# Three tiles of their own for two of a pair's seven split operands, and the last row tile's sums put ahead of the early products

## The chip, the cores and the metric

The kernel runs on one core of one Trainium2 chip. The metric is the device time of one launch in microseconds (us). A core has a matrix engine, TensorE (PE; its weight loads are listed apart as PEld), VectorE (DVE), ScalarE (ACT), GpSimd (POOL), a sync engine (SP) that issues transfers, and DMA engines. Each takes its instructions in the order in which they were put into its queue, and waits by semaphores for what the others do. Tiles lie in on-chip memory (SBUF); PE writes into banks of PSUM, which DVE and ACT read.

## What is computed

One layer of an encoder for a sequence of 1024 rows of width 1024 in float32: a norm, an input projection, an S5 scan beside a Fourier mixer, an output projection, and then the part that the change touches, a gated feed-forward network with a convolution of width 3 along the sequence:

```
h = h + concat([y_ssm, y_fft]) @ w_out
up = rmsnorm(h, g_ffn) @ w_up                      # 1024 x 1024  @  1024 x 5632
conv = conv_b + sum_k conv_w[k] * shifted(up, k)   # k = 0, 1, 2
gate, val = split(conv, 2)
h = h + (gelu(gate) * val) @ w_down                # 1024 x 2816  @  2816 x 1024
out = rmsnorm(h, g_final)
```

## The kernel before

**Precision.** A float32 product is made of three matmuls on float32r operands: each operand is split into a high part (a copy on ACT, L151) and a low part (a subtraction, on DVE, L152, or on POOL where the code says so), and high x high, high x low and low x high are summed (`mm`, L130).

**The stage of the output projection (`rows`, R0 to R7).** Row tile s, 128 rows, is multiplied by `w_out`, added to h, and its sum of squares is taken. **The norm and its transpose (`columns`, C0 to C7)** scale row tile s, transpose it on PE (L1033, tiles `n2_s_pt`), and put it, split, into the operands of the up-projection: row tiles 0 to 3 into `B11` and `B21` (tile `xa`); row tiles 4 to 7 into sums with the row tile four places ahead of them (L1049 to L1053) and from there into `T1` (tile `t1o`), `T2` (`t2o`), `T3` and `B22` (`xb`) and `T4` (`t4o`). The split into T4 is on POOL, that into T1 too, except for the last row tile.

**The up-projection (`up_pair`, 22 pairs j).** Pair j is 128 columns of the gate and the 128 of the value, with 1024 rows. Its four blocks are worked out with seven products in place of eight, after Strassen and Winograd: `weights(j)` loads four blocks `wu` of `w_up`, makes from them three sums `ws` on DVE (L1083, L1084, L1086; a fourth, L1085, goes into a `wu` tile), and splits the seven operands 0 to 6 (A11, S2, A12, A21, S1, A22, S4) into tiles `wo{j}_0` to `wo{j}_6`. Each product is 12 matmuls of 128x512, so a pair has 84. Products 0 and 2 go into bank `u1`, 1 into `u2`, 3 and 5 into `u3`, 4 and 6 into `u4`. DVE and ACT add the banks up (L1116, L1119, L1137 to L1147), convolve (L1099, L1102), apply gelu (L1150) and multiply (L1151), and SP writes the result to memory as `adr{j}`.

**Early products (`early_pair`, E0 to E4).** For pairs 0 to 4, products 0 and 2 need `xa` alone, that is row tiles 0 to 3. They are made ahead, from operands `we{j}_0` and `we{j}_1`, while the last row tiles are still normed; these pairs then have 60 matmuls left. Results are kept in `ug{j}`; those of pairs 2 to 4 lie in the ring of `wd_tile`.

**Buffers.** A ring is a set of buffers that tiles of one tag take in turn; who wants one waits until the readers of its old tile are done. All split operands of `w_up` (tag `wp`) share a ring of five (`NWP`), the blocks as loaded (tag `st`) one of five, and the sums `ws` one of three. `wd_tile` is a ring of three tiles of the size of a split operand. Blocks of `w_out` lie in it, then `ug2` to `ug4`; after pair 4 it is idle until `load_first`, which is called ahead of pair 21 and loads and splits six blocks for the down projection (`first0` to `first5`), the last two into this ring.

**Order.** `SEQ2` says in which order R, C and E are written. The order of each engine's queue is then made by a scheduler that plans with a timeline of its own: a changed line can move instructions at other places too, and pairs interleave (products 2, 5 and 6 of pair j are run by PE inside pair j + 1).

After the 22 pairs the down projection runs (banks `pd`), two halves of four row tiles.

Of the kernel before, what the change touches and what calls it, by code (L numbers as in the profile page):

```python
# [12 lines left out]
F32R = mybir.dt.float32r  # L13
# [7 lines left out]
P = 128  # L21
# [12 lines left out]
NWP = 5  # L34
# [1 line left out]
NTAB = 1026  # L36
NT4 = 9
MODE = "x"
SEQ2 = "R0 R1 C0 R2 C1 R3 C2 R4 C3 R5 C4 R6 R7 E0 C5 E1 C6 E2 E3 E4 C7"


ON = {
# [47 lines left out]
def encoder_block(  # L90
# [8 lines left out]
    V, A, PE, GP = nc.vector, nc.scalar, nc.tensor, nc.gpsimd  # L99
# [5 lines left out]
    outer = ctx.enter_context(tc.tile_pool(name="outer", bufs=1))  # L105
# [44 lines left out]
    def split(dst_hi, dst_lo, src, eng=V):  # L150
        A.activation(dst_hi, src, AF.Copy)  # L151
        return eng.tensor_sub(dst_lo, src, dst_hi.bitcast(F32))  # L152
# [759 lines left out]
    def w_out_block(part, n, k, dst=None):  # L912
        r0 = part * 512 + k * P
        return load_split(w_out[0][r0:r0 + P, n * 512:(n + 1) * 512], 1, f"wo{part}_{n}_{k}", dst,
                          opt(f"wo{part}{n}{k}", V))
# [44 lines left out]
    def raw(name):  # L960
        return x16.tile([P, 512], F32, name=name, tag="ra", bufs=3)

    def wd_tile(name):
        return fp.tile([P, 2, 512], F32R, name=name, tag="wd", bufs=3)
# [32 lines left out]
    wo = [[w_out_block(0, n, k, wd_tile(f"wot{n}_{k}") if n and k else None) for k in range(4)] for n in range(2)]  # L997
# [69 lines left out]
    def weight_block(j, i, kh, name):  # L1067
        c0 = i * D_FF + j * P
        t = outer.tile([P, 512], F32, name=name, tag="st", bufs=5)
        st_load(nc.sync.dma_start(t.rearrange("p (k c) -> p k c", k=4),  # L1070
                                  w_up[0][:, c0:c0 + P].rearrange("(k p) c -> p k c", p=P)[:, 4 * kh:4 * kh + 4]))
        return t

    def operand(t, name, e=V):
        w = outer.tile([P, 2, 512], F32R, name=name, tag="wp", bufs=NWP)
        split(w[:, 0], w[:, 1], t, e)
        return w.rearrange("p t (k c) -> p t k c", k=4)

    def weights(j, early):

        A11, A12, A21, A22 = (weight_block(j, i, kh, f"wu{j}_{i}{kh}") for i in range(2) for kh in range(2))
        S1, S2, S4 = (raw(f"ws{j}_{i}") for i in (1, 2, 4))
        V.tensor_add(S1, A21, A22)  # L1083
        V.tensor_sub(S2, S1, A11)  # L1084
        V.tensor_sub(A21, A11, A21)  # L1085
        V.tensor_sub(S4, A12, S2)  # L1086
        return [None if early and i in (0, 2) else operand(t, f"wo{j}_{i}")
                for i, t in enumerate((A11, S2, A12, A21, S1, A22, S4))]

    def product(dst, w, xx, fresh, more=False):  # L1090
# [30 lines left out]
    def early_pair(j):  # L1121
        w11, w12 = (operand(weight_block(j, 0, kh, f"we{j}_{kh}"), f"we{j}_{kh}_o") for kh in range(2))
        done[j] = t4(f"ug{j}") if j < 2 else wd_tile(f"ug{j}").rearrange("p i c -> p (i c)").bitcast(F32)
        for _ in first_half(j, done[j], w11, w12):
            pass

    def up_pair(j):
        w11, w2, w12, w3, w1, w22, w4 = weights(j, j in done)
        b2, b3, b4 = bank(f"u2_{j}"), bank2(f"u3_{j}"), bank2(f"u4_{j}")
        cv = t4(f"uv{j}")  # L1130
        u2, p7 = halves(f"up_{j}")
        cg = done[j] if j in done else t4(f"ug{j}")
        if j not in done:
            fh = first_half(j, cg, w11, w12)
            next(fh)
        product(b2, w2, T2, True)
        V.tensor_add(u2, cg[:, 512:1024], b2)  # L1137
        if j not in done:
            next(fh, None)
        product(b3, w3, T3, True, True)  # L1140
        V.tensor_add(p7, u2, b3)
        product(b4, w1, T1, True, True)
        V.tensor_add(cv[:, 512:1024], p7, b4)
        product(b3, w22, T4, False, True)
        V.tensor_add(cv[:, 0:512], u2, b3)
        product(b4, w4, B22, False, True)
        V.tensor_add(cg[:, 512:1024], u2, b4)  # L1147
        g = conv(cg, j, f"cg{j}")
        v = conv(cv, NFF + j, f"cv{j}")
        A.activation(g, g, AF.Gelu_apprx_tanh)  # L1150
        V.tensor_mul(g, g, v)  # L1151
        nc.sync.dma_start(adr[j], g)

    steps = {"R": rows, "C": columns, "E": early_pair}
    for tok in SEQ2.split():
        n2_end = steps[tok[0]](int(tok[1:]))
# [146 lines left out]
```

## Time and profile before

| | |
|---|---|
| time, median of 3 runs | 1111.56 us (1110.78 to 1112.57) |
| the profiled execution | 1111.17 us, its span 1109.4 us |
| mean clock granted to PE | 0.971 of full speed |
| early products and last row tiles | up to about 452 us |
| pairs 0 to 21 | about 447 to 867 us |
| down projection | about 867 us to the end |

A timeline row has the start in us, the duration in us, the engine, the line, the operation, the tiles as output<-inputs (buffer numbers left out, so `wo10_0` is `wo`), the shape and how many instructions the row joins; in brackets how long the engine was idle before it, and who released it.

The rows of the queues that are shown with the change have no times; where they carry names in full, `wo10_0_5475` is operand 0 of pair 10 (the last number is a mere count).

### The profile page before, as it was taken

Reading aid. Unit: us, or ns where it says so; the run is one execution under the profiler, and the core shown is the slowest. Engines: PE = TensorE matmul, PEld = TensorE weight load, DVE = VectorE, ACT = ScalarE, POOL = GpSimd, SP = SyncE. Lnnn points to the kernel's source line nnn. Section 1 sums busy time; section 2 is a strip of 40 time slices with the busy share of each in tenths; the row PEclk is TensorE's granted clock in tenths of the full one; section 3 lists DMA queues with packets and bytes.
Section 4 is the critical chain, followed back from the end, with each engine's and each line's share of the span. In section 5 each row is a group of like instructions: output and inputs, shape, how many; then the busy total and the mean of one; then the engine's idle time right before and its main releaser. Section 6 shows DMA issues by size and latency. Waiting matters only on the chain.

```text
span 1109.4 us, 13600 instructions
## 1 busy us (share of the span) xinstructions
PE 1005.3 (91%) x4636; PEld 820.9 (74%) x4636; DVE 869.2 (78%) x1599; ACT 449.4 (41%) x819; POOL 232.2 (21%) x245
## 2 busy tenths in 40 slices
PE   2799887788799997899999999999989999999997
PEld 1677765666678886688777777777768788888885
DVE  6998989999897898699887887878887733483335
ACT  5443232532126464344443434435344433353333
POOL 6257565775650022000000000000000000010002
PEclk9999888887999999899999999999999999999999
DMA  7251002431012332223222232222330774366521
GB/s 232 39 162 51 22 22 85 145 118 57 25 39 92 108 124 76 66 86 104 87 87 76 67 105 67 80 82 66 100 109 19 245 272 146 116 225 221 162 95 76
DMA packets 115259, 115.25 MB, mean 104 GB/s; under 512 B 17217, under 2 KB 85878, under 8 KB 115190
## 3 DMA queue, kind: packets, MB, share of 16 engines
q1 hardware_dynamic: 115046, 114.06, 32.4%
q8 instruction: 36, 0.59, 0.2%
q14 instruction: 33, 0.27, 0.1%
q10 hardware_dynamic: 144, 0.33, 0.1%
HBM read 91.82 MB, written 22.51 MB: 103 GB/s over the span
## 4 chain that ended last, share of the span: by engine, by line
PE 53%; DVE 4%; DMA 2%; ACT 1%; issue 1%; POOL 0%; POOLq 0%; DVEq 0%; ACTq 0%
PE u L130 31%; PE pd L130 21%; DMA wu<-in_w_up_dram 1%; DVE cg L1102 1%; DVE wo L152 1%; ACT wo L151 1%; DVE cv L1102 1%; ACT cg L1099 0%; DVE first L152 0%; DMA first_st<-adr 0%; DMA first_st<-in_w_down_dram 0%; DVE ws L1086 0%; DVE ug L1147 0%; DVE up L1137 0%; DVE ws L1084 0%
## 5 line engine op out<-in xcount | busy, mean ns | idle before, releaser
L130 PE MATMUL pd<-wd,at 128*128 128x512 f32 x1008 | 229.1, 389 | 2.6 <-ACT wd L151 1.6
L130 PEld LDWEIGHTS pd<-wd,at 128*128 128x128 f32 x1008 | 189.0, 188 | 42.6 <-ACT wd L151 2.0
L1201 POOL TENSOR_TENSOR o<-hb,gl 128x512 f32<-128x512 f32 (+1 forms) x10 | 13.4, 1343 | 640.6 <-DVE hb L1197 635.4
L130 PE MATMUL u<-xb,wo 128*128 128x512 f32 x528 | 130.2, 392 | 0.0
L130 PEld LDWEIGHTS u<-xb,wo 128*128 128x128 f32 x528 | 98.2, 188 | 24.0 <-DVE wo L152 4.0
L130 PE MATMUL u<-xa,wo 128*128 128x512 f32 x408 | 102.6, 394 | 6.7 <-ACT wo L151 5.6
L152 DVE TENSOR_TENSOR at<-at_st,at 128x512 fp32r<-128x512 f32 x42 | 29.0, 691 | 100.5 <-ACT at L151 100.4
L151 ACT ACTIVATE wo<-wu 128x512 fp32r<-128x512 f32 x78 | 49.3, 632 | 130.4 <-PE u L130 125.1
L130 PEld LDWEIGHTS u<-xa,wo 128*128 128x128 f32 x408 | 75.4, 188 | 28.1 <-ACT wo L151 11.1
L130 PE MATMUL pin<-xh,win 128*128 128x512 f32 x256 | 78.2, 406 | 1.1 <-ACT xh L224 1.1
L130 PE MATMUL u<-t2o,wo 128*128 128x512 f32 x264 | 69.3, 400 | 9.2 <-ACT t2o L151 8.3
L151 ACT ACTIVATE wo<-ws 128x512 fp32r<-128x512 f32 x66 | 41.3, 625 | 74.7 <-PE u L130 67.2
L130 PE MATMUL u<-t1o,wo 128*128 128x512 f32 x264 | 69.1, 391 | 1.8 <-ACT wo L151 1.8
L151 ACT ACTIVATE at<-at_st 128x512 fp32r<-128x512 f32 x42 | 26.4, 629 | 106.3 <-PE pd L130 97.7
L1102 DVE SCALAR_TENSOR_TENSOR cg<-ug,cw,cg 128x896 f32<-128x896 f32 (+1 forms) x88 | 62.0, 746 | 8.7 <-ACT cg L1099 8.7
L130 PEld LDWEIGHTS u<-t2o,wo 128*128 128x128 f32 x264 | 49.6, 192 | 22.6 <-ACT t2o L151 8.7
L130 PE MATMUL u<-t4o,wo 128*128 128x512 f32 x264 | 63.5, 389 | 0.0
L1102 DVE SCALAR_TENSOR_TENSOR cv<-uv,cw,cv 128x896 f32<-128x896 f32 (+1 forms) x88 | 62.0, 744 | 0.0
L130 PEld LDWEIGHTS u<-t1o,wo 128*128 128x128 f32 x264 | 49.2, 188 | 13.4 <-ACT wo L151 3.4
L130 PE MATMUL pwo<-wo,yf 128*128 128x512 f32 x192 | 52.0, 420 | 7.6 <-DVE h L928 4.3
L152 DVE TENSOR_TENSOR wo<-wu,wo 128x512 fp32r<-128x512 f32 x78 | 53.5, 685 | 5.9 <-ACT wo L151 5.8
L152 DVE TENSOR_TENSOR wd<-wd_st,wd 128x512 fp32r<-128x512 f32 x84 | 55.8, 698 | 2.4 <-ACT wd L151 2.3
(357 smaller groups left out, 1964.8 us busy)
## 6 DMA issues: line engine op xcount, KB each, us to landing
wu<-in_w_up_dram SPq DMA_DIRECT2D x88, 256.0 KB, 2.9
wd_st<-in_w_down_dram SPq DMA_DIRECT2D x84, 256.0 KB, 3.7
adr<-cg SPq DMA_DIRECT2D x22, 512.0 KB, 2.6
at_st<-adr SPq DMA_DIRECT2D x42, 256.0 KB, 3.9
xr<-in_x_dram SPq DMA_DIRECT2D x8, 512.0 KB, 8.1
win_st<-in_w_in_dram SPq DMA_DIRECT2D x16, 256.0 KB, 3.0
wo_st<-in_w_out_dram SPq DMA_DIRECT2D x16, 256.0 KB, 2.9
h<-in_x_dram SPq DMA_DIRECT2D x8, 512.0 KB, 4.6
```

Source lines behind the costliest of these rows:

```text
L130: i = PE.matmul(o, lhsT, rhs, start=start, stop=stop, skip_group_check=skip)
L151: A.activation(dst_hi, src, AF.Copy)
L152: return eng.tensor_sub(dst_lo, src, dst_hi.bitcast(F32))
L1102: V.scalar_tensor_tensor(cv[:, lo:hi], src[:, at:at + hi - lo], w, cv[:, lo:hi], ALU.mult, ALU.add)
L1201: GP.tensor_mul(o[:, sl], hv[:, sl], gl[:, sl])
```

## The change

Two edits:

```
-SEQ2 = "R0 R1 C0 R2 C1 R3 C2 R4 C3 R5 C4 R6 R7 E0 C5 E1 C6 E2 E3 E4 C7"
+SEQ2 = "R0 R1 C0 R2 C1 R3 C2 R4 C3 R5 C4 R6 R7 E0 C5 C6 C7 E1 E2 E3 E4"
```

```
-    def operand(t, name, e=V):
-        w = outer.tile([P, 2, 512], F32R, name=name, tag="wp", bufs=NWP)
+    def operand(t, name, w=None, e=V):
+        if w is None:
+            w = outer.tile([P, 2, 512], F32R, name=name, tag="wp", bufs=NWP)
         split(w[:, 0], w[:, 1], t, e)
         return w.rearrange("p t (k c) -> p t k c", k=4)
...
-        return [None if early and i in (0, 2) else operand(t, f"wo{j}_{i}")
+        return [None if early and i in (0, 2) else operand(t, f"wo{j}_{i}", wd_tile(f"wx{j}_{i}") if j > 4 and i in (1, 4) else None)
                 for i, t in enumerate((A11, S2, A12, A21, S1, A22, S4))]
```

The first writes the norm, transposes, sums and splits of row tiles 6 and 7 ahead of the early products of pairs 1 to 4. The second takes operands 1 and 4 (S2 and S1) of pairs 5 to 21 out of the ring of five and puts them, as `wx{j}_1` and `wx{j}_4`, into the ring of `wd_tile`. No operation is added or removed. Lines behind the edit have a number one higher after it. SP issues the same transfers; only `adr0` and two blocks of pair 21 change places with a neighbour, and POOL's queue has the same order.

**Where the queues differ: the last row tile.** On DVE, before, from the first sum of pair 1's weights (`ws_1_4263`) on; `n_7_pt` are row tile 7's transposes, `h_2712` and `h_2310` its sums:

```order
L1083 TENSOR_TENSOR ws_1_4263<-wu_10_4259,wu_11_4261 128x512
L152 TENSOR_TENSOR wo_4_4161<-ws_1_4148,wo_4_4161 128x512
L1085 TENSOR_TENSOR wu_10_4259<-wu_00_4255,wu_10_4259 128x512
L1084 TENSOR_TENSOR ws_2_4264<-ws_1_4263,wu_00_4255 128x512
L152 TENSOR_TENSOR wo_5_4164<-wu_11_4146,wo_5_4164 128x512
L1050 TENSOR_TENSOR h_2712<-n_7_pt_4114,h_2712 128x512
L1051 TENSOR_TENSOR h_2310<-n_7_pt_4120,h_2712 128x512
L1052 TENSOR_TENSOR h_2310<-n_7_pt_4120,h_2310 128x512
L152 TENSOR_TENSOR t1o<-h_2712,t1o 128x4x128
L152 TENSOR_TENSOR wo_6_4167<-ws_4_4150,wo_6_4167 128x512
L152 TENSOR_TENSOR t2o<-h_2310,t2o 128x4x128
```

The same place of DVE after the change, from the first sum of pair 0's weights (`ws_1_4148`) to the first of pair 1's, with rows of pair 0 left out between:

```order
L1084 TENSOR_TENSOR ws_1_4148<-wu_10_4144,wu_11_4146 128x512
L1050 TENSOR_TENSOR h_2712<-n_7_pt_3962,h_2712 128x512
L152 TENSOR_TENSOR t2o<-h_2465,t2o 128x4x128
...
L1051 TENSOR_TENSOR h_2310<-n_7_pt_3968,h_2712 128x512
L1052 TENSOR_TENSOR h_2310<-n_7_pt_3968,h_2310 128x512
...
L152 TENSOR_TENSOR t1o<-h_2712,t1o 128x4x128
...
L152 TENSOR_TENSOR t2o<-h_2310,t2o 128x4x128
...
L1084 TENSOR_TENSOR ws_1_4263<-wu_10_4259,wu_11_4261 128x512
```

Row tile 7's sums and its splits now stand ahead of pair 1's `ws`, mixed with row tile 6's. On PE the same place before, from the last products of the early pairs on:

```order
L130 MATMUL u1_3_4047<-xa_3367,we3_1_o_4043 128x512 x12
L130 MATMUL u1_4_4085<-xa_3367,we4_0_o_4076 128x512 x2
L1033 MATMUL n2_7_pt0_4114<-ident_70,n2_7_xs_4112 128x128
L1033 MATMUL n2_7_pt1_4120<-ident_70,n2_7_xs_4112 128x128 x4
L130 MATMUL u1_4_4085<-xa_3367,we4_1_o_4081 128x512 x12
L130 MATMUL u2_0_4170<-t2o_3172,wo0_1_4155 128x512 x12
L130 MATMUL u3_0_4171<-xb_3368,wo0_3_4158 128x512
L130 MATMUL u4_0_4172<-t1o_3370,wo0_4_4161 128x512 x12
L130 MATMUL u3_0_4171<-xb_3368,wo0_3_4158 128x512 x11
```

And after:

```order
L1033 MATMUL n2_7_pt0_3962<-ident_70,n2_7_xs_3960 128x128 x4
L1033 MATMUL n2_7_pt1_3968<-ident_70,n2_7_xs_3960 128x128 x4
L130 MATMUL u1_2_4037<-xa_3367,we2_1_o_4033 128x512 x12
L130 MATMUL u1_3_4075<-xa_3367,we3_0_o_4066 128x512
L130 MATMUL u1_4_4113<-xa_3367,we4_0_o_4104 128x512 x12
L130 MATMUL u1_3_4075<-xa_3367,we3_1_o_4071 128x512 x12
L130 MATMUL u2_0_4170<-t2o_3172,wo0_1_4155 128x512
L130 MATMUL u3_0_4171<-xb_3368,wo0_3_4158 128x512
L130 MATMUL u1_4_4113<-xa_3367,we4_1_o_4109 128x512 x12
L130 MATMUL u4_0_4172<-t1o_3370,wo0_4_4161 128x512 x2
L130 MATMUL u2_0_4170<-t2o_3172,wo0_1_4155 128x512 x11
```

The transposes have moved ahead of four early groups, and single matmuls of pair 0 (`u2_0`, `u3_0`) stand ahead of the last early product.

**A steady pair.** PE before, from the fifth product of pair 10 to the first of pair 11:

```order
L130 MATMUL u3_9_5348<-t4o_3369,wo9_5_5341 128x512 x12
L130 MATMUL u4_10_5498<-t1o_3370,wo10_4_5487 128x512 x8
L130 MATMUL u4_9_5349<-xb_3368,wo9_6_5344 128x512 x12
L130 MATMUL u4_10_5498<-t1o_3370,wo10_4_5487 128x512 x2
L130 MATMUL u1_11_5651<-xa_3367,wo11_0_5624 128x512 x2
L130 MATMUL u2_11_5645<-t2o_3172,wo11_1_5627 128x512 x2
```

And after:

```order
L130 MATMUL u3_10_5497<-xb_3368,wo10_3_5484 128x512 x10
L130 MATMUL u3_9_5348<-t4o_3369,wo9_5_5341 128x512 x12
L130 MATMUL u4_9_5349<-xb_3368,wo9_6_5344 128x512 x12
L130 MATMUL u1_11_5651<-xa_3367,wo11_0_5624 128x512 x2
L130 MATMUL u2_11_5645<-t2o_3172,wx11_1_5627 128x512 x12
```

The copy into `wo11_0` waits, before, for the product of `wo9_6`, whose buffer it takes, and PE has two matmuls of `u4_10` between that product and `u1_11`. After, it takes the buffer of `wo9_5`, and the twelve matmuls of `wo9_6` lie between. The copies of ACT for pair 12 before:

```order
L151 ACTIVATE wo11_6_5642<-ws11_4_5619 128x512
L151 ACTIVATE wo12_0_5773<-wu12_00_5758 128x512
L151 ACTIVATE wo12_1_5776<-ws12_2_5767 128x512
L1099 ACTIVATE cg10_5594<-ug10_5501,cw_107 128x1024
L1099 ACTIVATE cv10_5600<-uv10_5499,cw_107 128x1024
L1116 ACTIVATE ug11_5650<-u1_11_5651 128x512
L151 ACTIVATE wo12_2_5779<-wu12_01_5760 128x512
```

And after:

```order
L151 ACTIVATE wo11_6_5642<-ws11_4_5619 128x512
L151 ACTIVATE wx12_1_5776<-ws12_2_5767 128x512
L151 ACTIVATE wx12_4_5785<-ws12_1_5766 128x512
L151 ACTIVATE wo12_0_5773<-wu12_00_5758 128x512
L151 ACTIVATE wo12_2_5779<-wu12_01_5760 128x512
L1100 ACTIVATE cg10_5594<-ug10_5501,cw_107 128x1024
```

The copies of the sums, `wx12_1` and `wx12_4`, now stand ahead of `wo12_0`.

**Pair 20 and the first blocks of the down projection.** ACT before; `first` is the tile of blocks 0 to 3:

```order
L151 ACTIVATE first_7099<-first0_st_7102 128x512
L151 ACTIVATE first_7099<-first1_st_7106 128x512
L151 ACTIVATE wo20_0_6965<-wu20_00_6950 128x512
L151 ACTIVATE wo20_1_6968<-ws20_2_6959 128x512
L1099 ACTIVATE cg18_6786<-ug18_6693,cw_107 128x1024
```

And after:

```order
L151 ACTIVATE first_7099<-first0_st_7102 128x512
L151 ACTIVATE wo20_0_6965<-wu20_00_6950 128x512
L151 ACTIVATE wo20_2_6971<-wu20_01_6952 128x512
L151 ACTIVATE first_7099<-first1_st_7106 128x512
L1100 ACTIVATE cg18_6786<-ug18_6693,cw_107 128x1024
...
L151 ACTIVATE first_7099<-first2_st_7110 128x512
L151 ACTIVATE first_7099<-first3_st_7114 128x512
L151 ACTIVATE first0_7100<-first4_st_7118 128x512
L151 ACTIVATE wo20_3_6974<-wu20_10_6954 128x512
```

Pair 20's `wo20_0` has moved ahead of `first1`, and `wo20_3` now stands behind `first1` to `first4`.

## Prediction

> **What bounds the kernel now.** I read the busy shares first, then TensorE's (PE's) timeline around its idle times, then the engines that it waits for there.
>
> ```profile
> PE 1005.3 (91%) x4636; PEld 820.9 (74%) x4636; DVE 869.2 (78%) x1599; ACT 449.4 (41%) x819; POOL 232.2 (21%) x245
> ```
>
> PE is the bound: no other engine comes near its 91%. The change removes no matmul, so it can only win where PE waits. In the stretch that the change touches first, PE's timeline and its windows (columns: stretch, length, busy time of PE, weight loads, VectorE (DVE), ScalarE (ACT) and GpSimd (POOL), then the granted clock, the DMA share and GB/s) read:
>
> ```profile
> 433.12 0.71 PE L1033 MATMUL n_pt<-ident,n_xs 128*128 128x128 f32 x5
> 435.42 3.02 PE L130 MATMUL u<-xa,we_o 128*128 128x512 f32 x12 [1.60 <-ACT ug L1116]
> 446.69 0.79 PE L130 MATMUL u<-t2o,wo 128*128 128x512 f32 x1 [8.26 <-ACT t2o L151]
> 448.41 4.17 PE L130 MATMUL u<-t2o,wo 128*128 128x512 f32 x11 [0.92 <-DVE t2o L152]
> 452.41 0.39 PE L130 MATMUL u<-xb,wo 128*128 128x512 f32 x1
> ```
>
> ```profile
> 434.00:438.00 4.00, 2.58 (x11) 2.17 (x12) 2.31 (x3) 2.37 (x5) 0.56 (x1) 1.00 0.39 115
> 438.00:442.00 4.00, 0.43 (x2) 0.01 (x1) 1.24 (x3) 0.00 (x0) 0.00 (x0) 0.89 0.21 59
> 442.00:446.00 4.00, 0.00 (x0) 0.00 (x0) 3.90 (x8) 1.51 (x3) 0.67 (x1) 0.50 0.34 101
> 446.00:450.00 4.00, 2.39 (x5) 1.59 (x6) 4.00 (x5) 2.16 (x5) 1.87 (x2) 0.50 0.11 32
> ```
>
> PE finishes the last early product at 438.4 and idles 8.26 us for `t2o` of row tile 7, then 0.92 us for its low half, and the clock that follows the hole is 0.50. I call this the **transition**. VectorE's and GpSimd's timelines tell why:
>
> ```profile
> 429.25 1.78 DVE L152 TENSOR_TENSOR t2o<-h,t2o 128x512 fp32r<-128x512 f32 x1
> 430.94 0.68 DVE L1084 TENSOR_TENSOR ws<-ws,wu 128x512 f32<-128x512 f32 x1
> 431.55 0.68 DVE L1085 TENSOR_TENSOR wu<-wu,wu 128x512 f32<-128x512 f32 x1
> ...
> 440.76 0.69 DVE L1083 TENSOR_TENSOR ws<-wu,wu 128x512 f32<-128x512 f32 x1 [4.45 <-DMA wu<-in_w_up_dram]
> ...
> 443.77 0.68 DVE L1050 TENSOR_TENSOR h<-n_pt,h 128x512 f32<-128x512 f32 x1
> ...
> 447.67 0.68 DVE L152 TENSOR_TENSOR t2o<-h,t2o 128x512 fp32r<-128x512 f32 x1
> ```
>
> ```profile
> 428.74 1.73 POOL L1053 TENSOR_TENSOR h<-h,h 128x512 f32<-128x512 f32 x1
> ```
>
> Pair 1's `ws` waits 4.45 us for its weight DMA, in order, ahead of row tile 7's sums (L1050 at 443.77), whose inputs the PE had transposed by 433.83 (433.12 + 0.71).
>
> The second loss returns with **every pair** of the up-projection. A steady piece of PE's timeline, the copy of ScalarE that ends its wait, and the waits from 560 to 780:
>
> ```profile
> 649.81 0.74 PE L130 MATMUL u<-xa,wo 128*128 128x512 f32 x2 [0.27 <-ACT wo L151]
> ...
> 655.46 2.88 PE L130 MATMUL u<-xa,wo 128*128 128x512 f32 x12
> 658.18 3.08 PE L130 MATMUL u<-xb,wo 128*128 128x512 f32 x12
> ...
> 669.69 0.73 PE L130 MATMUL u<-xa,wo 128*128 128x512 f32 x2 [0.27 <-ACT wo L151]
> ```
>
> ```profile
> 669.00 0.63 ACT L151 ACTIVATE wo<-wu 128x512 fp32r<-128x512 f32 x1 [3.90 <-PE u L130]
> ```
>
> ```profile
> ACT wo L151 <- PE u L130: 113.7, 55, 4.1
> ```
>
> A period is 669.69 - 649.81 = 19.88 us. A product without a stall takes 658.18 - 655.46 = 2.72 us, 0.2267 us a matmul, so 84 matmuls could take 19.04: about 0.83 us is lost. The loss begins where PE needs `wo_0` of the next pair, whose copy ACT starts only at 669.00, since PE has just freed its slot. The four stretches after the transition, in windows:
>
> ```profile
> 468.70:540.60 71.90, 70.78 (x310) 57.72 (x309) 71.81 (x111) 35.19 (x45) 0.00 (x0) 1.00 0.30 95
> 452.41:570.25 117.84, 115.52 (x505) 94.12 (x503) 103.28 (x158) 48.97 (x66) 0.00 (x0) 1.00 0.27 85
> 570.25:788.23 217.98, 215.24 (x923) 170.87 (x924) 182.07 (x275) 92.85 (x131) 0.00 (x0) 1.00 0.25 80
> 788.23:867.17 78.94, 75.48 (x327) 60.68 (x327) 60.33 (x91) 33.68 (x47) 0.00 (x0) 1.00 0.25 81
> ```
>
> At 0.2267 a matmul, the last three lose 117.84 - 505 x 0.2267 = 3.4 us, 217.98 - 924 x 0.2267 = 8.5 us (one record is missing there; 11 pairs have 924) and 78.94 - 327 x 0.2267 = 4.8 us. The down projection behind them loses nothing to win: window 880 to 1080 has PE busy all through.
>
> ```profile
> 880.00:1080.00 200.00, 200.00 (x884) 165.62 (x883) 91.07 (x165) 75.01 (x134) 6.83 (x4) 1.00 0.55 184
> ```
>
> **The change, part by part.** No operation is added or removed; order and buffers change.
>
> *Transition.* The order puts the transposes of row tile 7 directly behind those of 6, and its sums on VectorE ahead of pair 1's `ws`. L1050 of row tile 7 then stands at 429.25, and the split of `t2o` that PE needs is the 13th operation from there. Start to start they take 0.61 us (430.94 to 431.55): 7.9 us. Both sets of GpSimd work (L1053 and `t4o`, twice) now fall into this stretch. An operation with both inputs in SBUF beside one takes 1.78 instead of 0.68 us; three such holds add 3.3. So `t2o` is whole at about 429.25 + 7.9 + 3.3 = 440.4. PE meanwhile runs what it ran before: the 1.60 us wait for `ug` stays somewhere, and the last early product ends near 439.3, one late copy (about 0.95 us) behind 438.4. PE begins the remaining eleven `u2_0` matmuls at 440.4 and ends near 442.9; besides these it has done one matmul of `u3_0` and two of `u4_0`. Before, it had done as much 0.68 us after 452.41, at 453.1. Gain 10.2 us. From it I take 0.5 for pair 1. Its `ws` still waits for its last weight block, which is issued once the split of `wo0_3` (near 439.6) has freed a buffer, and needs 2.9 us in the median, 4.45 as VectorE saw it last:
>
> ```profile
> wu<-in_w_up_dram SPq DMA_DIRECT2D x88, 256.0 KB, 2.9
> ```
>
> Landed near 444, and seven VectorE steps of 0.61 later, `wo1_1` is split at about 448.4; PE would need it near 448. **9.7 us**. Bounds: 10.8 if nothing holds VectorE (PE's own work then ends it at 439.3), 5 if a second DMA wait of 4.45 us slips ahead.
>
> On the clock: after 8.26 us idle it was 0.50, and after 1.60 us idle (window 434 to 438) it stayed 1.00; my three short waits (1.6, 0.95, 1.1) leave it at 1.00. [...]
>
> *Pairs 5 to 20.* Seven operands shared five slots, so pair 11's `wo_0` waited for pair 9's last product (`wo9_6`), with two matmuls (0.45 us) left to cover a copy of 0.63. Now operands 1 and 4 have three slots of their own, and `wo11_0` waits for `u3_9<-wo9_5`: a product earlier, 2.72 us of cover against 0.63. I followed each wait of a period from its start, in matmuls of 0.2267 us: `wo_3` waits for the product of `wo_0`, which ends after 24 (5.4 us), is copied by 6.7 and needed after 36 (8.2); its low half comes by 9.3 and is needed after 50 (11.3). `ws` is ready near 11.7 (its last DMA waits for a split of the pair ahead); `wo_6` waits for 60 matmuls (13.6); `wx_1` and `wx_4` follow it and are copied by 16.1; `wo_0` waits for 72 (16.3), is copied by 17.6 and needed after 84 (19.0). VectorE has 182.07 / 11 = 16.6 us of work in 19.04. No wait is left, so of 8.5 us I take **8.2**. Bounds: 8.5, and 0 if another wait replaces it.
>
> *Pairs 0 to 4 and the crossing, 452 to 570.* The early pairs' buffers do not change, and VectorE is full there (71.81 of 71.90). Only stalls from pair 5 on, and one or two by order, go: **1.6 us** of 3.4 (bounds -1 and 3).
>
> *Tail.*
>
> ```profile
> 810.73 0.73 PE L130 MATMUL u<-xa,wo 128*128 128x512 f32 x2 [2.17 <-ACT wo L151]
> 820.43 0.73 PE L130 MATMUL u<-t1o,wo 128*128 128x512 f32 x2 [0.75 <-ACT wo L151]
> ```
>
> ```profile
> 809.52 0.63 ACT L151 ACTIVATE first<-first_st 128x512 fp32r<-128x512 f32 x1 [3.45 <-DMA first_st<-in_w_down_dram]
> 810.06 0.61 ACT L151 ACTIVATE wo<-wu 128x512 fp32r<-128x512 f32 x1
> ```
>
> The first `w_down` blocks stand in ACT's queue, and `first1` made pair 20's `wo_0` late (2.17 us). Now `wo20_0` and `wo20_2` stand ahead of it, and pair 20's `wx` are split sooner. But `wo20_3` stands behind four such copies, with almost no slack, and `first4` and `first5` take two of the three slots, so `wx21_4` has to wait for `wx21_1`'s product (slack about 3 us). Of 4.8 us I take **3.5** (bounds 0 and 4.8).
>
> Sum: 9.7 + 8.2 + 1.6 + 3.5 = 23.0 us. The profiled run took 1111.17 us (span 1109.4 and 1.8 around it), 0.39 under the median of 1111.56. 1111.17 - 23.0 = **1088.2 us**. With all upper bounds, 10.8 + 8.5 + 3 + 4.8 = 27.1: 1084; with what the walk may have overlooked in wins, 1081.
>
> **The rivals.**
> - *The steady wait is replaced.* The `wx` copies wait on `ws`, thus on a DMA, and stand ahead of `wo_0` in ACT's queue; PE would wait for the same copy for another reason. For it: VectorE's 4.45 us wait for `wu` above. Against: `ws` at 11.7 could be 3 us later before `wo_0` misses 19.0. It gives 1111.2 - 9.7 - 1.6 - 3.5 = 1096.4.
> - *VectorE becomes the bound in pairs 0 to 4* and the transition's gain is given back there. For it: 71.81 of 71.90 busy. Against: it is VectorE that waited before (4.45, idle again until 468), and its sums and splits move up with PE's. Given back whole: 1111.2 - 1.6 - 8.2 - 3.5 = 1097.9; by half: 1093.
> - *The clock drops all the same* in the transition. For it: 0.50 lasted from 442 to 450. Against: 1.00 after 1.60 us. Some eight matmuls at half clock cost 8 x 0.2267 = 1.8 us: 1090.0.
> - *The queue turns on PE (slower).* The same ACT order as in the first rival, but with the DMA later than the 3 us of slack: `wo_0` then comes late in each of 16 pairs. It decides once the loss in each pair exceeds 0.83 by (9.7 + 1.6 + 3.5 + 2.2) / 16 = 1.06 us, thus 1.9 us a pair, or a landing 5 us later than read. At 2.5 us a pair: 1111.2 - 14.8 + 16 x 1.67 = 1123. The DMA share of 0.25 speaks against it.
> - *It does little*: the waits are refilled on both sides, 1111.
>
> **How the numbers follow.** Forecast 0.56 (1088.2; own range 1084 to 1092), steady wait replaced 0.13 (1096), VectorE gives back 0.15 (1093 to 1098), clock 0.06 (1090), better than my bounds 0.03, little 0.04 and slower 0.03. The range, 1082 to 1099, holds 0.9 of these as priced; I leave it there, since the middle cases' prices are rough. 0.2% (2.2 us) is about what a measurement of this kernel can tell from no change: faster 0.93, same 0.04, slower 0.03.
>
> **What would show it.** Right: no PE idle of over 2 us between 430 and 450 and a clock of 1.00 through it; L1050 of row tile 7 near 429; the first `u2_0` group done by 443; pair periods of 19.0 to 19.1 us without an ACT `wo` wait; pair 20 starting without the 2.17 us. Wrong: periods still near 19.8, a DMA or VectorE wait in front of `wx` or `wo1_1`, or PE idle between 445 and 540.

## Result and the profile after

The changed kernel takes 1085.65 us, median of 4 runs (1084.58 to 1087.14), against 1112.07 (1110.78 to 1113.18) before: a ratio of 0.9764, 95% interval 0.9747 to 0.9781. The forecast was 1088.2, the range 1082 to 1099. The profiled execution took 1085.37 us with a span of 1083.6, 25.8 us less than that of before.

TensorE (PE) around the transition after the change, its timeline and then its windows:

```profile
431.97 3.02 PE L130 MATMUL u<-xa,we_o 128*128 128x512 f32 x12 [1.47 <-ACT ug L1117]
434.83 0.39 PE L130 MATMUL u<-t2o,wo 128*128 128x512 f32 x1
435.38 0.50 PE L130 MATMUL u<-xb,wo 128*128 128x512 f32 x1 [0.17 <-ACT xb L151]
435.87 3.02 PE L130 MATMUL u<-xa,we_o 128*128 128x512 f32 x12
...
439.68 2.83 PE L130 MATMUL u<-t2o,wo 128*128 128x512 f32 x11 [0.34 <-DVE t2o L152]
442.35 2.66 PE L130 MATMUL u<-xb,wo 128*128 128x512 f32 x11
```

```profile
434.00:438.00 4.00, 3.83 (x16) 2.65 (x15) 4.00 (x6) 3.86 (x8) 2.02 (x2) 1.00 0.21 61
438.00:442.00 4.00, 3.66 (x16) 2.67 (x16) 4.00 (x6) 1.11 (x2) 0.47 (x1) 1.00 0.43 127
```

The first matmul of `u2_0` has no wait where it had 8.26 us, that of `u3_0` has 0.17, and the other eleven of `u2_0` have 0.34 where they had 0.92. The early products run under VectorE's (DVE's) sums, and the clock stays at 1.00. VectorE's timeline shows the sums at their new place, and four holds beside GpSimd's work (1.18, 1.75, 1.41 and 1.78 instead of 0.68):

```profile
428.33 0.68 DVE L1050 TENSOR_TENSOR h<-n_pt,h 128x512 f32<-128x512 f32 x1
428.93 1.18 DVE L152 TENSOR_TENSOR t2o<-h,t2o 128x512 fp32r<-128x512 f32 x1
...
430.63 1.75 DVE L1086 TENSOR_TENSOR wu<-wu,wu 128x512 f32<-128x512 f32 x1
...
434.10 1.41 DVE L152 TENSOR_TENSOR xb<-h,xb 128x512 fp32r<-128x512 f32 x1
...
437.24 1.78 DVE L152 TENSOR_TENSOR wo<-wu,wo 128x512 fp32r<-128x512 f32 x1
438.95 0.68 DVE L152 TENSOR_TENSOR t2o<-h,t2o 128x512 fp32r<-128x512 f32 x1
```

Behind it, two starts of a pair and two windows, from 442.35 to the start of pair 8 and from there to that of pair 19:

```profile
575.11 0.62 PE L130 MATMUL u<-xa,wo 128*128 128x512 f32 x2
...
594.15 0.62 PE L130 MATMUL u<-xa,wo 128*128 128x512 f32 x2
```

```profile
442.35:556.07 113.72, 113.72 (x503) 93.96 (x502) 106.50 (x165) 50.02 (x67) 0.00 (x0) 1.00 0.31 95
556.07:765.51 209.44, 209.44 (x926) 173.42 (x925) 182.12 (x275) 94.71 (x132) 0.00 (x0) 1.00 0.28 83
```

A period is 594.15 - 575.11 = 19.04 us, and PE is busy in every part of 323 us. What is left to lose lies in pairs 20 and 21 and ahead of the down projection, whose own waits (1.57 and 1.02 us) are as before:

```profile
805.86 2.56 PE L130 MATMUL u<-xa,wo 128*128 128x512 f32 x10 [0.90 <-DVE wo L152]
```

The same work, found in both timelines, tells where the 25.8 us were gained:

| from | before, us | after, us | ahead by | gained |
|---|---|---|---|---|
| first matmul of the early products (the same code up to here) | 406.47 | 405.57 | 0.9 | 0.9 |
| eleven `u2_0`, one `u3_0` and two `u4_0` matmuls done | 453.1 | 442.35 | 10.7 | 9.8 |
| pair 8 starts | 570.30 | 556.07 | 14.2 | 3.5 |
| pair 19 starts | 788.94 | 765.51 | 23.4 | 9.2 |
| the long run of the down projection starts | 874.55 | 848.79 | 25.8 | 2.3 |

The first 0.9 us come from code that is equal in both kernels, so they belong to the execution and not to the change.

### The profile page after: what moved, and what is told of

Its sections match the earlier page's. It is cut to its first block, busy times and chain, and to the rows that moved or that the text cites. A ratio compares the mean times of both kernels' runs of the same rounds, so it can differ in the third digit from the quotient of the medians.

```text
span 1083.6 us, 13600 instructions
## 1 busy us (share of the span) xinstructions
PE 999.4 (92%) x4636; PEld 823.8 (76%) x4636; DVE 865.6 (80%) x1599; ACT 450.8 (42%) x819; POOL 231.5 (21%) x245
## 4 chain that ended last, share of the span: by engine, by line
PE 55%; DVE 3%; issue 1%; DMA 1%; ACT 1%; POOL 0%; POOLq 0%; DVEq 0%; ACTq 0%
PE u L130 34%; PE pd L130 21%; DMA wu<-in_w_up_dram 1%; DVE cg L1103 0%; DVE wo L152 0%; ACT cg L1100 0%; DMA first_st<-in_w_down_dram 0%; DVE first L152 0%; DVE cv L1103 0%; DVE ws L1087 0%; DVE ug L1148 0%; DVE xb L152 0%; DVE ws L1085 0%; DVE t2o L152 0%; ACT cv L1100 0%
## 5 line engine op out<-in xcount | busy, mean ns | idle before, releaser
L130 PE MATMUL u<-xa,wo 128*128 128x512 f32 x408 | 98.8, 390 | 1.0 <-DVE wo L152 0.9
L1103 DVE SCALAR_TENSOR_TENSOR cg<-ug,cw,cg 128x896 f32<-128x896 f32 (+1 forms) x88 | 62.1, 745 | 13.9 <-ACT cg L1100 13.9
L151 ACT ACTIVATE at<-at_st 128x512 fp32r<-128x512 f32 x42 | 26.4, 629 | 107.2 <-PE pd L130 98.4
L1103 DVE SCALAR_TENSOR_TENSOR cv<-uv,cw,cv 128x896 f32<-128x896 f32 (+1 forms) x88 | 62.0, 744 | 0.0
L130 PEld LDWEIGHTS pin<-xh,win 128*128 128x128 f32 x256 | 50.2, 199 | 11.9 <-ACT xh L224 1.8
L151 ACT ACTIVATE wo<-ws 128x512 fp32r<-128x512 f32 x32 | 20.2, 630 | 89.5 <-PE u L130 83.8
L130 PEld LDWEIGHTS u<-t4o,wo 128*128 128x128 f32 x264 | 49.5, 188 | 10.3
L151 ACT ACTIVATE wd<-wd_st 128x512 fp32r<-128x512 f32 x84 | 49.2, 624 | 6.4 <-DMA wd_st<-in_w_down_dram 4.8
L130 PEld LDWEIGHTS pwo<-wo,yf 128*128 128x128 f32 x192 | 36.5, 198 | 17.3 <-DVE h L928 3.9
```

Of the source, the lines that this page charges most:

```text
L130: i = PE.matmul(o, lhsT, rhs, start=start, stop=stop, skip_group_check=skip)
L1103: V.scalar_tensor_tensor(cv[:, lo:hi], src[:, at:at + hi - lo], w, cv[:, lo:hi], ALU.mult, ALU.add)
```

## Experiments

Each run was timed beside runs of the kernel before on the same chip.

**The two edits apart.** The order alone:

```
-SEQ2 = "... R6 R7 E0 C5 E1 C6 E2 E3 E4 C7"
+SEQ2 = "... R6 R7 E0 C5 C6 C7 E1 E2 E3 E4"
```

> The order alone, with all seven operands in the ring of five. Theory (two separate gains): the hole before t2o of row tile 7 goes as in the changed kernel (the first full u2_0 group begins near 440 instead of 448.4, about 9.8 us of gain), while the pair period stays at 19.8 to 19.9 us and the 2.17 us wait of pair 20 for first1 stays. 1101 us (1099 to 1103). Rival (VectorE is full in pairs 0 to 4 and gives the gain back without the ring): 1106 to 1111 us.

1099.16 us against 1109.98; ratio 0.9908 (0.9893 to 0.9923). PE's timeline of this run:

```profile
440.78 2.79 PE L130 MATMUL u<-t2o,wo 128*128 128x512 f32 x11 [0.34 <-DVE t2o L152]
...
639.65 0.73 PE L130 MATMUL u<-xa,wo 128*128 128x512 f32 x2 [0.27 <-ACT wo L151]
...
659.51 0.73 PE L130 MATMUL u<-xa,wo 128*128 128x512 f32 x2 [0.27 <-ACT wo L151]
...
800.21 0.90 PE L130 MATMUL u<-xa,wo 128*128 128x512 f32 x2 [1.87 <-ACT wo L151]
...
801.76 3.51 PE L130 MATMUL u<-xa,wo 128*128 128x512 f32 x10
```

```profile
802.00:804.00 2.00, 2.00 (x6) 1.52 (x6) 2.00 (x3) 1.94 (x3) 0.00 (x0) 0.50 0.51 183
```

The hole is gone, the period is still 659.51 - 639.65 = 19.86, and pair 20 still waits for `first1`. Pair 8 starts at 560.18, 10.1 us ahead of the kernel before, and by medians 10.8 us arrive at the end, so VectorE, though full in pairs 0 to 4, gives nothing back. Behind the wait of 1.87 us the clock is at 0.50 from 800.6 to 804.1: 3.5 us at half speed (the ten matmuls from 801.76 on take 805.11 - 801.76 = 3.35 us to the next start instead of 2.27), which cost this execution, the longest of the four, about 1.7 us.

The ring alone, with the old `SEQ2` and the changed `operand`:

> The ring alone, with the old order. Theory: the hole of 8.26 us and the clock of 0.50 behind it stay; the pair period falls to 19.04 us from about pair 6 on, and pair 20 does not wait 2.17 us for first1: 9.3 + 2 to 3 + 2.3 us of gain, 1098 us (1096 to 1100). Rival (the steady gain comes from the way PE's rows interleave after the new order, not from the ring): 1107 us or more.

1095.78 us; ratio 0.9873 (0.9859 to 0.9888).

```profile
445.28 0.80 PE L130 MATMUL u<-t2o,wo 128*128 128x512 f32 x1 [7.85 <-ACT t2o L151]
446.99 4.53 PE L130 MATMUL u<-t2o,wo 128*128 128x512 f32 x11 [0.92 <-DVE t2o L152]
...
642.36 0.62 PE L130 MATMUL u<-xa,wo 128*128 128x512 f32 x2
...
661.40 0.62 PE L130 MATMUL u<-xa,wo 128*128 128x512 f32 x2
```

The hole stays and the period is 19.04; the time is a little below the 1096 to 1100 us that were expected. By medians the parts gain 10.8 and 14.2 us, 25.0 together; the whole change gained 26.4 in its first comparison and 25.2 in the later one. The edits add up, and neither needs the other.

**What in the ring counts.** First, only operand 1 leaves the ring of five:

```
-wd_tile(f"wx{j}_{i}") if j > 4 and i in (1, 4) else None
+wd_tile(f"wx{j}_{i}") if j > 4 and i == 1 else None
```

> New order, and only operand 1 in the idle ring; six operands share five tiles. Pair 11's wo_0 then still waits for pair 9's last product (wo9_6), as before the change, but PE has ten matmuls (2.27 us) of u4_10 left behind it, instead of two. Theory (what counts is the PE work that covers the copy of 0.63 us and its hand-overs, 0.9 us in all): period 19.04 us, 1085 to 1087 us. Rival (what counts is how many operands are taken out of the ring): half the gain, period 19.46 us, about 1090 us.

1085.70 us; ratio 0.9778 (0.9763 to 0.9792). Pairs start at

```profile
652.01 0.61 PE L130 MATMUL u<-xa,wo 128*128 128x512 f32 x2
...
671.05 0.61 PE L130 MATMUL u<-xa,wo 128*128 128x512 f32 x2
```

19.04 us apart. One operand gives the whole gain; the count of tiles is not what matters. What fits is the *cover*: the PE work that lies between the release of a buffer and the first use of its next tile. Then only operand 4 (`i == 4`):

> New order, and only operand 4 in the idle ring. wo_0 waits for wo_6 of two pairs ahead again, with five matmuls (1.13 us) left to cover it; the twelve matmuls of u1 then stand together, so that the low half is needed 1.6 us after the release, about when it comes. Theory of the cover: high half just in time, low half about 0.0 to 0.3 us late: period 19.05 to 19.35 us, 1086 to 1090 us, and a wait of PE or its weight loads for wo on DVE or ACT appears in each pair. Rival (number of operands): the same as with operand 1 alone, 19.46 us.

1095.19 us; ratio 0.9866 (0.9849 to 0.9882): worse than both theories said. PE and VectorE in one pair:

```profile
656.13 5.80 PE L130 MATMUL u<-xa,wo 128*128 128x512 f32 x24
661.77 0.61 PE L130 MATMUL u<-t2o,wo 128*128 128x512 f32 x2
662.58 2.57 PE L130 MATMUL u<-t2o,wo 128*128 128x512 f32 x10 [0.19 <-DVE wo L152]
...
675.86 5.40 PE L130 MATMUL u<-xa,wo 128*128 128x512 f32 x22
```

```profile
655.87 0.69 DVE L152 TENSOR_TENSOR wo<-wu,wo 128x512 fp32r<-128x512 f32 x1
657.26 1.41 DVE L1103 SCALAR_TENSOR_TENSOR cg<-ug,cw,cg 128x896 f32<-128x896 f32 x2 [0.70 <-ACT cg L1100]
658.59 1.41 DVE L1103 SCALAR_TENSOR_TENSOR cv<-uv,cw,cv 128x896 f32<-128x896 f32 x2
659.92 1.40 DVE L1103 SCALAR_TENSOR_TENSOR cg<-ug,cw,cg 128x127 f32<-128x127 f32 x2
...
661.84 0.68 DVE L152 TENSOR_TENSOR wo<-ws,wo 128x512 fp32r<-128x512 f32 x1
```

The weight loads (PEld) in the eleven pairs from 560 to 780 us, with total, count and longest wait:

```profile
PEld u L130 <- DVE wo L152: 9.7, 22, 0.6
```

The period is 675.86 - 656.13 = 19.73. PE does not wait for `wo_0`'s high half, as the cover of five matmuls said, and the low half is late by about as much as the theory had: the weight loads wait 0.29 us for it, and the first 24 matmuls take 661.77 - 656.13 = 5.64 us instead of 5.44. The larger part was not foreseen. Each pair has a second such wait: the low half of `wo_1` stands on VectorE behind six taps (terms of the convolution, L1103) and ends at 662.52, and PE stalls there. So the theory was incomplete: a second operand has to be covered too, on VectorE's side.

To tell "cover" from "it has to be operand 1", operands 0 and 2 took the idle ring (`i in (0, 2)`), and operand 1 stayed in the ring of five:

> New order, operands 0 and 2 in the idle ring in place of 1 and 4. The same two tiles' relief, other operands. After the run with operand 4 alone the theory is: both of a pair's first two operands, wo_0 and wo_1, need cover, the high half for the copy and the low half ahead of VectorE's convolution. Here PE takes whole groups of twelve and a group or more lies between each release and its use: period 19.04 to 19.1 us, 1085 to 1087 us. Rival (it must be operand 1 that leaves the ring, since its low half is caught behind the convolution): period 19.4 to 19.7 us, 1090 to 1095 us.

1090.39 us; ratio 0.9825 (0.9810 to 0.9840). In time this is the rival's lowest figure, in the profile it is not the rival:

```profile
661.78 5.60 PE L130 MATMUL u<-xa,wx 128*128 128x512 f32 x24
...
680.82 1.52 PE L130 MATMUL u<-xa,wx 128*128 128x512 f32 x6
```

```profile
801.36 4.61 PE L130 MATMUL u<-t4o,wo 128*128 128x512 f32 x12 [2.98 <-DVE up L1142]
818.05 0.73 PE L130 MATMUL u<-xa,wx 128*128 128x512 f32 x2 [1.21 <-ACT wx L151]
835.82 2.57 PE L130 MATMUL u<-xa,wx 128*128 128x512 f32 x10 [0.69 <-DVE wx L152]
```

```profile
802.00:804.00 2.00, 2.00 (x6) 1.58 (x5) 2.00 (x3) 0.00 (x0) 0.00 (x0) 0.50 0.06 25
```

The period is 19.04 with operand 1 in the ring of five, so cover it is. What this run lacks is lost in the last pairs: PE idles 2.98, 1.21 and 0.69 us, and behind the first of these the clock is at 0.50 from 801.9 to 805.4, so that twelve matmuls take 805.81 - 801.36 = 4.45 us instead of 2.72. Four tiles (`first4`, `first5` and the pair's own two) want the ring of three there. That this is the cause was not tested, and the longest wait ends with a sum on VectorE (L1142), not with a tile of the ring.

**What in the order counts.** `C7` ahead of `E4` alone, with the old ring:

```
-SEQ2 = "... R6 R7 E0 C5 E1 C6 E2 E3 E4 C7"
+SEQ2 = "... R6 R7 E0 C5 E1 C6 E2 E3 C7 E4"
```

> Old ring; C7 written ahead of E4 only. VectorE then has row tile 7's sums and splits ahead of pair 1's ws, as after the change, but TensorE's queue has the twelve matmuls of u2_0 ahead of the last early product (twelve matmuls), which can no longer fill the wait. Theory (the gain needs both: sums early, and early products left to run under them): t2o whole near 439 to 440, PE idle for 3 to 4 us before it, then 2.7 us of early product still to do, so about 3 us less gain than the full order: on the scale where the order alone took 1099.2 us and the kernel before 1110.0, 1102 us (1101 to 1104). Rival (VectorE's order carries the whole gain): 1099 us.

1103.90 us; ratio 0.9945 (0.9929 to 0.9962), at the upper end.

```profile
436.34 0.50 PE L130 MATMUL u<-t2o,wo 128*128 128x512 f32 x1 [2.75 <-ACT t2o L151]
438.79 5.04 PE L130 MATMUL u<-t2o,wo 128*128 128x512 f32 x11 [1.94 <-DVE t2o L152]
...
446.67 2.88 PE L130 MATMUL u<-xa,we_o 128*128 128x512 f32 x12
```

```profile
434.00:438.00 4.00, 0.50 (x1) 0.19 (x1) 4.00 (x6) 2.34 (x5) 1.28 (x1) 0.86 0.22 66
438.00:442.00 4.00, 3.21 (x8) 2.54 (x9) 3.91 (x7) 1.82 (x4) 1.59 (x1) 0.50 0.26 70
```

VectorE has the sums early (`t2o` whole at 438.74), but the early product that should fill the wait stands behind it in PE's queue, at 446.67. PE idles 2.75 and 1.94 us, and the clock falls to 0.50 behind the first of these: the eleven matmuls take 5.04 us instead of 2.83. Early sums alone gave 5.7 us of the 10.8: early products have to be left to run under them.

**What the slow clock cost.** The kernel before, with 36 extra matmuls in the hole whose result nobody reads:

```
+    fill = bank("fill")
+    for r in range(3):
+        for k in range(4):
+            for wi, xi in ((0, 0), (0, 1), (1, 0)):
+                mm(fill, B11[:, wi, k, 0:P], B21[:, xi, k], start=(k == 0 and wi == 0 and xi == 0),
+                   stop=(k == 3 and wi == 1))
```

> The kernel before with 36 extra matmuls (8.2 us), whose result nobody reads, in the hole ahead of u2_0; VectorE's order there is that of before. Theory (the hole costs its wait and, behind it, the half clock): the clock stays at 1.00 from 438 to 452, t2o is whole at 448.4 as before, u2_0 ends near 450.9 instead of 452.6: about 1.5 us faster in spite of 36 more matmuls, 1108.5 us where before is 1110. Rival (the clock of 0.50 has another cause, or the fill delays what follows): clock still 0.50 near 448, same time or slower.

1105.87 us against 1109.56; ratio 0.997 (0.996 to 0.998).

```profile
434.30 0.71 PE L1033 MATMUL n_pt<-ident,n_xs 128*128 128x128 f32 x5
...
447.77 2.79 PE L130 MATMUL u<-t2o,wo 128*128 128x512 f32 x11 [1.36 <-DVE t2o L152]
450.39 2.88 PE L130 MATMUL u<-xb,wo 128*128 128x512 f32 x12
```

```profile
446.00:450.00 4.00, 2.64 (x11) 1.95 (x12) 4.00 (x5) 2.52 (x5) 1.85 (x2) 1.00 0.05 13
```

The scheduler put 22 of the 36 ahead of the last early product and 14 behind it. The clock holds, and the eleven matmuls take 450.39 - 447.77 = 2.62 us from start to next start, where the kernel before took 452.41 - 448.41 = 4.00: the slow clock cost 1.4 us there. VectorE in this run:

```profile
440.69 0.69 DVE L1083 TENSOR_TENSOR ws<-wu,wu 128x512 f32<-128x512 f32 x1 [3.17 <-DMA wu<-in_w_up_dram]
...
447.03 0.68 DVE L152 TENSOR_TENSOR t2o<-h,t2o 128x512 fp32r<-128x512 f32 x1
```

The run gained more than the expected 1.5, some 3.2 us from the transposes to this place (450.39 - 434.30 = 16.1 against 452.41 - 433.12 = 19.3), since `t2o` was also split 1.8 us sooner after the transposes (447.03 - 434.30 = 12.7 against 447.67 - 433.12 = 14.6): `wo0_6` no longer stands ahead of it on VectorE (0.6 us), and the DMA wait was 3.17 us instead of 4.45. That transfer took 3.0 us from issue to landing (437.55 to 440.57), and 4.3 in the kernel before (436.33 to 440.63); that the extra matmuls had a part in this is not shown.

**The tail.** The call of `load_first` was put behind pair 21's weights, first with operand 1 alone:

```
     def up_pair(j):
         w11, w2, w12, w3, w1, w22, w4 = weights(j, j in done)
+        if j == NFF - 1:
+            load_first()
...
-        if j == NFF - 1:
-            load_first()
         up_pair(j)
```

> New order, only operand 1 in the idle ring, and the six first blocks of the down projection called behind pair 21's weights instead of ahead of them. Theory of the tail (the low halves of first0 to first4 stand ahead of wo20_3's on VectorE, which holds a weight buffer, so pair 21's last block is loaded late: 0.9 us): that wait and the 0.6 us before it go, pair 21 may wait for first blocks instead: 1084 to 1085.5 us where operand 1 alone took 1085.7. Rival (the blocks are then late for the matmuls that fill pair 21): 1086 to 1089 us.

1084.24 us; ratio 0.9769 (0.9754 to 0.9783); the waits of 0.2 us in pair 20 and 0.90 in pair 21 are gone, and one of 0.72 us stands among the matmuls that fill pair 21. Whether it beats the changed kernel was tried with both on one chip, and with the late call in the changed kernel itself:

> The changed kernel itself, on the chip of the two runs beside it: 1084 to 1086 us where before is 1109 to 1112; PE loses 0.2 + 0.9 us in pairs 20 and 21.

> Operand 1 alone in the idle ring and the first blocks called behind pair 21's weights, timed beside the changed kernel. Theory of the tail: 1.0 to 1.7 us faster than the changed kernel, 1083 to 1084.5 us. Rival (the difference to the changed kernel so far is one between chips): the same within 0.5 us.

> The changed kernel (operands 1 and 4) with the late call of the first blocks. If the tail's loss is the low halves of the first blocks ahead of wo20_3's alone, it gains as much as with operand 1 alone, 1083 to 1084.5 us; if the two tiles that first4 and first5 hold are a cost of their own, pair 21 loses 1 us or more and it stays at 1085 us or above.

| | median, us | ratio to before (interval) |
|---|---|---|
| changed kernel | 1085.68 | 0.9773 (0.9759 to 0.9786) |
| operand 1 alone, late call | 1085.01 | 0.9767 (0.9754 to 0.9781) |
| both operands, late call | 1085.61 | 0.9772 (0.9759 to 0.9786) |

The three cannot be told apart; the gain of 1.0 to 1.7 us that the theory of the tail gave is not there. The wait moves: PE waits 0.77 us for ScalarE (ACT) among the filling matmuls in the second kernel, and 1.01 us behind them in the third. In this execution of the changed kernel pair 21 waits 0.26 us where it waited 0.90 in the first. The second kernel's row, then the changed kernel's:

```profile
813.97 0.97 PE L130 MATMUL pd<-first 128*128 128x512 f32 x3 [0.77 <-ACT ug L1120]
```

```profile
805.82 2.60 PE L130 MATMUL u<-xa,wo 128*128 128x512 f32 x10 [0.26 <-DVE wo L152]
```

The last weight block of pair 21 took 3.6 us from issue to landing here (797.83 to 801.38) and 4.2 in the first execution (797.23 to 801.41). So pair 21 went on at 805.8 in both, though PE came 0.6 us later here.

No kernel that was run is shown to be faster than the changed one.

## Why the prediction was right

**Transition: 9.7 us forecast, 9.8 measured.** The walk holds step by step. `t2o` was forecast whole at 440.4 and was at 438.95 + 0.68 = 439.6 in an execution that ran 0.9 us ahead. Three holds of 1.1 us were assumed; four measured 0.50 + 1.07 + 0.73 + 1.10 = 3.4. PE's three waits are 1.47, 0.17 and 0.34. That the two figures are so close is in part luck. To the point that was measured the walk had 10.2 us, 0.4 more than came, since the eleven matmuls began and ended a little later than it said; the 0.5 us taken off for `wo1_1` was not due, as PE has no wait there, and made up for it.

**Clock.** By the run with the filled hole, 1.4 of these 9.8 us are the clock's. The changed kernel's short waits (1.47, 0.17 and 0.34 us) left it at 1.00. The eight matmuls at half clock, 1.8 us, that the rival on the clock was priced with were my estimate, and no run shows them in the transition of the new order: in seven executions with this order, the changed kernel's two among them, the longest wait there is 1.47 to 1.56 us, and the twelve matmuls behind it take 2.85 to 2.90 us from start to next start, 2.86 in the changed kernel's first, whose clock was 1.00. But the margin was smaller than "1.00 after 1.60 us" made it look: in the order alone a wait of 1.87 us was followed by 0.50.

**Pairs 0 to 7: 1.6 forecast, 3.5 measured.** I let a full VectorE keep half of the waits. In fact PE is busy throughout the window from 442.35 to 556.07. The order alone shows this too: its gain is not given back.

**Steady pairs: 8.2 forecast, 9.2 measured.** The period is 19.04, as worked out. The size was off because my window ended at 788.23, ahead of the last period's stall; from start to start, 11 periods before were 788.94 - 570.30 = 218.6 us, a loss of 9.2. The mechanism was told too simply: I put the loss down to `wo_0`'s high half alone. Operand 4 alone relieves that half and still loses 0.7 us a pair: 0.2 since the low half of `wo_0` is late, the rest at the low half of `wo_1`. What the change does is to give both of a pair's first two operands time; operand 1 alone is enough for it.

**Tail: 3.5 forecast, 2.3 measured.** The 2.17 us wait for `first1` went. The doubt about `wo20_3` was in place: the copies of the first blocks stand ahead of it, its low half, which VectorE ends at 797.20, frees the last weight buffer late (its block is issued at 797.23), and pair 21 loses 0.90 us, and 0.26 in the second execution.

The sum, 23.0 against 24.9 (25.8 less the 0.9 of equal code), was short for two terms that were sized too low, the early pairs by 1.9 and the steady pairs by 1.0; the tail, sized 1.2 too high, hid a part of it. Of the rivals, none came: the `wx` copies did not hold `wo_0`, VectorE gave nothing back, and the clock stayed. The slower case needed `wo_0` late in every pair, and no pair from 442 to 765 us has a wait at all.

## What to carry to other kernels

When operands rotate through a ring, look for the work that lies between the release of a buffer and the need of its next tile, for both halves of every operand at the head of a group; with two matmuls of 0.23 us against a copy of 0.63 each pair paid 0.8 us, and one operand taken out of the ring cured it. When a late stage's inputs come from an in-order engine, put their work ahead of what waits for a DMA there (4.45 us on VectorE here), and keep ready matmuls in PE's queue to run meanwhile: early sums without them gave half (5.7 of 10.8 us). Before counting a loss per period, measure from start to start.

## What the runs showed of the hardware

**Behind an idle time of 1.87 us PE's clock fell to 0.50, and behind one of 2.17 us it stayed at 1.00.** Three runs have 0.50 behind short idle times. In the order alone it came at 800.6, 0.4 us behind one of 1.87 us; in the run with operands 0 and 2 at 801.9, 0.5 us behind one of 2.98; in the partial order at 436.8, behind one of 2.75 us and a single matmul, and ahead of the 1.94 us. In the kernel before, 2.17 us in pair 20 left the clock at 1.00, as did the transition's waits in the new order (1.47 us in the changed kernel) and 1.36 us in the filled hole. So the length of one idle time does not decide alone; what else does was not tested. The stretches at 0.50 lasted 3.5, 3.5, 6.9 us (partial order) and 10.3 (the kernel before, 441.1 to 451.4).

**Four VectorE operations that began beside one of GpSimd's ended 0.54 to 0.55 us after it.** In the changed kernel's transition these four held operations end at 430.11, 432.38, 435.51 and 439.02, and the GpSimd operations beside them at 429.56, 431.84, 434.96 and 438.47. The held ones have both inputs in SBUF; L1050, which reads PSUM, took 0.68 us beside the first of these GpSimd operations. Alone, one takes 0.60 us from start to start.

That 36 useless matmuls make a kernel faster (0.997, interval 0.996 to 0.998) was foreseen in its sign. Of the 3.2 us that the profiled execution gained there, 1.4 are the clock's; the rest came from VectorE's side and was not foreseen.
